# A LoRA projection: longer first loads, and GpSimd takes every second rounding

## The chip, the cores and the metric

The kernel runs on one core of a Trainium2 chip. The metric is the device time of one execution in microseconds (us). The kernel before took 163.57, 163.68 and 163.86 us in three runs; the median is 163.68 us. A core has five engines: TensorE (PE in the profile), VectorE (DVE), ScalarE (ACT), GpSimd (POOL) and SyncE (SP), which here does nothing but issue transfers and wait. Sixteen DMA engines move data between the chip's memory (HBM) and the on-chip buffer (SBUF).

## What is computed

```python
x_flat = x.reshape(-1, in_dim)            # 32768 x 256, float32
y = x_flat @ W                            # W: 256 x 256
lora_out = x_flat @ lora_A                # 256 x 16
lora_out = lora_out * lora_E              # 16 factors
lora_out = lora_out @ lora_B              # 16 x 256
y = y + scale * lora_out
```

The input is 33.6 MB and the output is as large. Everything else is small.

## The kernel before, in words

The kernel first folds the low-rank part into the weight: `weff = W + lora_A diag(lora_E) lora_B`, rounded to bf16 (lines 177 to 191 on VectorE, 238 to 246 on TensorE). After that, each output row is one product of an input row with `weff`.

The 32768 input rows are laid over 128 partitions, so a partition holds 256 rows of 256 numbers. "Rows" below means these: 8 rows are 1 MB of float32. They are cut into blocks (`BLOCKS`, line 11), and inside a block each partition's rows lie side by side in HBM, so that a load of n rows reads n KB in one piece for each partition (`rows_of`, line 97).

All rows go through one SBUF buffer, `ring`, which has room for 184 of the 256 rows (line 12). A load writes rows into the ring, the computation replaces them there by the results, and a store takes the results out. The last 72 rows use the places of the first 72, so their loads wait until the stores of those have landed.

The order of all large transfers is written out in `ORDER` (line 13): `L16` is a load of the next 16 rows, `S64` a store of the next 64, `W` the load of the weight. SyncE issues them in this order on one queue (lines 129 to 143). Before a load it waits for the stores whose places it takes (line 137); before a store it waits until ScalarE has counted up `s_c` (line 140). At the end it waits for the last stores (line 263). Every load has a semaphore of its own, `s_load`.

The computation goes in 32 steps of 8 rows, in two alternating sets of buffers:

- `rounded(n)` (line 158), on VectorE: round 8 rows from the ring to bf16, into `xb` (the cast of line 167). At the first step of a load it waits for that load (line 166).
- `transposes` (line 216), on TensorE: eight transposes (line 212) of `xb` into PSUM, `pt`. The two bf16 halves of a 32-bit word travel together, as float32.
- `copied(n)` (line 169), on VectorE: copy `pt` to SBUF, `xt` (line 172).
- `products` (line 222), on TensorE: sixteen products (line 228) of `xt` with `weff` into PSUM, `py`, in two halves of four rows.
- ScalarE copies each half from `py` back into the ring (line 202), and at the end of a store's rows it drains and counts up `s_c` (line 204).

TensorE's order is transposes of step n+1, then products of step n. So the results of step n come only after the input of step n+1 is there. VectorE's order is `copied(n)`, then `rounded(n+2)` (lines 193 to 195). GpSimd only builds the identity matrix for the transposes (lines 145 and 147) at the start.

Of the kernel before, what the change touches and what calls it, by code (L numbers as in the profile page):

```python
# [10 lines left out]
BLOCKS = [64, 32, 64, 24, 40, 32]  # L11
RING = 184
ORDER = [
    "L8", "W", "L8", "L16", "L16", "L16", "L16", "L16", "L24", "L24", "L16", "L24",
    "S64", "S32",
    "L8", "L16", "L16", "L16", "L16",  # L16
    "S64", "S24", "S40", "S32",
# [1 line left out]
G = 8  # L19
# [4 lines left out]
def kernel(  # L24
# [10 lines left out]
    nc = tc.nc  # L35
# [25 lines left out]
    xbs = [const.tile([P, G, K], BF16, name=f"xb_{i}") for i in range(2)]  # L61
# [23 lines left out]
    s_load = {f: sem(f"load_{f}") for f, _ in loads}  # L85

    s_last = sem("stores")
    s_store = {f: sem(f"store_{f}") for f, _ in stores if f < ROWS - RING}
# [4 lines left out]
    s_t, s_m, s_c = sem("s_t"), sem("s_m"), sem("s_c")  # L93
    k_x, k_t, k_y = ([sem(f"{k}_{i}") for i in range(2)] for k in ("k_x", "k_t", "k_y"))
    s_setup = sem("s_setup")

    def rows_of(flat, f, n):
        first, rows = block_of[f]
        block = flat[first * P:(first + rows) * P, :].rearrange("(p b) k -> p b k", b=rows)
        return block[:, f - first:f - first + n, :]  # L100

    def place(f, n):
        return ring[:, f % RING:f % RING + n, :]

    steps = list(range(0, ROWS, G))
    NS = len(steps)
# [5 lines left out]
    def load(f, n):  # L112
        return nc.sync.dma_start(out=place(f, n), in_=rows_of(x_flat, f, n)).then_inc(s_load[f], 16)
# [12 lines left out]

    with tc.tile_critical():  # L127

        for kind, f, n in queue[1:]:
            if kind == "W":  # L130
                nc.sync.dma_start(
                    out=w_sb, in_=W.rearrange("(p c) m -> p c m", c=KC)
                ).then_inc(s_w, 16)
            elif kind == "L":
                for g, m in stores:
                    if g < f + n - RING and f - RING < g + m and g in s_store:
                        nc.sync.wait_ge(s_store.pop(g), 16)
                load(f, n)
            elif kind == "S":
                nc.sync.wait_ge(s_c, stores.index((f, n)) + 1)  # L140
                nc.sync.dma_start(out=rows_of(out_flat, f, n), in_=place(f, n)).then_inc(
                    s_store.get(f, s_last), 16
                )

        nc.gpsimd.memset(ident_f, 0.0).then_inc(s_setup, 1)  # L145
        nc.gpsimd.wait_ge(s_setup, 1)
        nc.gpsimd.affine_select(  # L147
            out=ident_f,
            in_=ident_f,
            compare_op=mybir.AluOpType.not_equal,  # L150
            fill=1.0,
            base=0,
            pattern=[[-1, P]],
            channel_multiplier=1,
        ).then_inc(s_setup, 1)


        def rounded(n):

            if n == NS:  # L160

                nc.vector.sem_inc(k_x[n % 2], 1)
            if n >= NS:
                return
            if steps[n] in s_load:
                nc.vector.wait_ge(s_load[steps[n]], 16)
            nc.vector.tensor_copy(out=xbs[n % 2], in_=place(steps[n], G)).then_inc(k_x[n % 2], 1)  # L167

        def copied(n):

            nc.vector.wait_ge(s_t, n + 1)
            nc.vector.tensor_copy(  # L172
                out=xts[n % 2].rearrange("p g r c -> p (g r c)"),
                in_=pts[n % 2].rearrange("p g r -> p (g r)").bitcast(BF16),
            ).then_inc(k_t[n % 2], 1)

        nc.vector.wait_ge(s_in, 48)
        nc.vector.tensor_copy(out=b_bf, in_=b_sb)  # L178
        nc.vector.wait_ge(s_setup, 3)
        nc.vector.tensor_scalar(  # L180
            out=ate,
            in0=ps_at,
            scalar1=e_sb,
            scalar2=float(scale),
            op0=mybir.AluOpType.mult,
            op1=mybir.AluOpType.mult,
        ).then_inc(s_setup, 1)
        rounded(0)
        nc.vector.wait_ge(s_w, 16)
        nc.vector.wait_ge(s_setup, 5)  # L190
        nc.vector.tensor_add(out=weff, in0=w_sb, in1=ps_aeb).then_inc(s_setup, 1)  # L191
        rounded(1)
        for n in range(NS):
            copied(n)
            rounded(n + 2)


        for k in k_y:
            nc.scalar.sem_inc(k, 1)
        for h in range(ROWS // H):  # L200
            nc.scalar.wait_ge(s_m, h + 1)
            nc.scalar.copy(out=place(h * H, H), in_=pys[h % 2]).then_inc(k_y[h % 2], 1)  # L202
            if (h + 1) * H in store_ends:
                nc.scalar.drain().then_inc(s_c, 1)  # L204


        def take(token):
            nc.tensor.wait_ge(token, 1).then_inc(token, -1)  # L208


        def transpose(b, j):
            return nc.tensor.transpose(  # L212
                pts[b][:, j, :], xbs[b][:, j, :].bitcast(FP32), ident_f
            )

        def transposes(b):
            take(k_x[b])
            for j in range(G):
                t = transpose(b, j)
            t.then_inc(s_t, 1)  # L220

        def products(b):
            take(k_t[b])
            for j in range(G):
                if j % H == 0:
                    take(k_y[j // H])
                for c in range(KC):
                    m = nc.tensor.matmul(  # L228
                        pys[j // H][:, j % H, :],
                        xts[b][:, j, :, c],  # L230
                        weff[:, c, :],
                        start=(c == 0),
                        stop=(c == KC - 1),
                    )
                if j % H == H - 1:
                    m.then_inc(s_m, 1)

        nc.tensor.wait_ge(s_setup, 2)
        nc.tensor.wait_ge(s_in, 48)
        for c in range(KC):  # L240
            t = nc.tensor.transpose(ps_at[:, c, :], a_sb[:, c, :], ident_f)  # L241
        t.then_inc(s_setup, 1)
        nc.tensor.wait_ge(s_setup, 4)
        for c in range(KC):
            m = nc.tensor.matmul(ps_aeb[:, c, :], ate[:, c, :], b_bf, start=True, stop=True)  # L245
        m.then_inc(s_setup, 1)
        transposes(0)
        nc.tensor.wait_ge(s_setup, 6)
        left = nc.tensor.alloc_register("left")
        nc.tensor.reg_mov(left, NS // 2)  # L250
        with nc.tensor.While(left):
            transposes(1)
            products(0)
            transposes(0)
            products(1)
            nc.tensor.reg_sub(left, left, 1)

        total = nc.sync.alloc_register("total")
        nc.sync.reg_mov(total, n_last)
# [39 lines left out]
```

## Time and profile before

| What | Value |
| --- | --- |
| profiled execution, whole | 163.49 us |
| its span on the engines | 161.7 us |
| median of three runs | 163.68 us |
| TensorE, matmuls | 91.0 us busy (56%), 780 instructions |
| VectorE | 76.4 us busy (47%), 67 instructions |
| ScalarE | 63.1 us busy (39%), 65 instructions |
| GpSimd | 0.7 us busy, 6 instructions |
| VectorE's casts, line 167 | 32 of 1220 ns |
| VectorE's copies, line 172 | 32 of 1221 ns |
| data moved | 67.42 MB, mean 417 GB/s over the span |
| DMA packets | 3522 |

The span runs from the first to the last instruction of the profile; the whole execution has 1.8 us more around it. The page gives, for each engine, how long it was busy, the busy share in 40 equal slices of the span, the DMA queues, the chain of work that ended last, and groups of like instructions with their mean duration and the idle time before them. Views of the trace behind the page give the same by time: the order of one engine's instructions, what it waited for, and sums over chosen stretches. "X <- Y" in a list of waits reads "X waited for Y". SPq is SyncE's queue of commands, ACTq ScalarE's.

### The profile page before, as it was taken

To read this page: it belongs to the slowest core of one execution; us is meant where nothing else is said; L and a number is where in the kernel's file an instruction comes from. 1 tells how busy PE (TensorE), PEld (TensorE's weight loads), DVE (VectorE), ACT (ScalarE), POOL (GpSimd) and SP (SyncE) were. 2 spreads that over 40 slices of the span, in tenths; PEclk is the share of its full clock that TensorE was granted. 3 is DMA by queue.
4 is the path that set the end of the run, shared out by engine and by line. 5 is a ranking of instruction groups with operands and counts; after the bars stand their busy time and mean duration, and the time that the engine had idled before them with its cause. 6 is when DMAs were issued, how large, how long until landed. Compare 5 with 4: busy or idle time off the path is not lost. (4 is left out here: it accounts for less than half of the span.)

```text
span 161.7 us, 1972 instructions
## 1 busy us (share of the span) xinstructions
PE 91.0 (56%) x780; PEld 81.5 (50%) x780; DVE 76.4 (47%) x67; ACT 63.1 (39%) x65; POOL 0.7 (0%) x6
## 2 busy tenths in 40 slices
PE   0188999999999999970000079999994000000000
PEld 0066899999799999960000066999993000000000
DVE  0296999985889988800000048999930000000000
ACT  3004486868586868680000005768685000000000
POOL 1000000000000000000000000000000000000000
PEclk9999999999999999996555558999999555555555
DMA  5999999999999999799699999999899799899992
GB/s 179 417 426 450 413 434 442 417 458 426 432 415 438 432 521 456 324 519 470 300 413 407 440 421 446 424 421 571 357 486 470 340 395 488 381 466 442 405 421 113
DMA packets 3522, 67.42 MB, mean 417 GB/s; under 512 B 560, under 2 KB 576, under 8 KB 704
## 3 DMA queue, kind: packets, MB, share of 16 engines
q1 hardware_dynamic: 3312, 67.37, 97.6%
q10 hardware_dynamic: 208, 0.03, 0.1%
q14 instruction: 2, 0.02, 0.0%
HBM read 33.85 MB, written 33.55 MB: 417 GB/s over the span
## 5 line engine op out<-in xcount | busy, mean ns | idle before, releaser
L202 ACT COPY ring<-py 128x1024 f32<-128x1024 f32 x64 | 61.8, 1017 | 58.6 <-PE py L228 58.5
L228 PE MATMUL py<-weff,xt 128*128 128x256 bf16 x512 | 62.2, 275 | 0.7 <-PEq L208 0.7
L228 PEld LDWEIGHTS py<-weff,xt 128*128 128x128 bf16 x512 | 50.5, 99 | 7.4 <-issue 1.5
L167 DVE CAST xb<-ring 128x2048 bf16<-128x2048 f32 x32 | 39.0, 1220 | 31.8 <-DMA ring<-in_x_dram 31.5
L212 PE MATMUL pt<-ident_f,xb 128*128 128x128 f32 x264 | 36.7, 286 | 24.0 <-PEq L208 23.9
L212 PEld LDWEIGHTS pt<-ident_f,xb 128*128 128x128 f32 x264 | 31.7, 148 | 25.9 <-issue 25.6
L172 DVE COPY xt<-pt 128x2048 bf16<-128x2048 bf16 x32 | 39.1, 1221 | 4.5 <-PE pt L212 4.4
L241 PE MATMUL py<-ident_f,a_sb 128*16 128x128 f32 x2 | 0.6, 396 | 6.8 <-DMA b_sb<-in_lora_B_dram 6.8
L241 PEld LDWEIGHTS py<-ident_f,a_sb 128*16 128x16 f32 x2 | 0.1, 88 | 6.8 <-issue 6.8
L178 DVE CAST b_bf<-b_sb 16x256 bf16<-16x256 f32 x1 | 0.3, 282 | 6.7 <-DMA b_sb<-in_lora_B_dram 6.7
L202 ACT ACT_TABLE_LOAD x1 | 1.3, 1283 | 2.4 <-issue 2.4
L245 PE MATMUL py<-b_bf,ate 16*128 16x256 bf16 x2 | 0.6, 402 | 0.6 <-DVE ate L180 0.6
L180 DVE TENSOR_SCALAR ate<-py,e_sb 16x256 bf16<-16x256 f32 x1 | 0.5, 472 | 0.5 <-PE py L241 0.5
L191 DVE TENSOR_TENSOR weff<-w_sb,py 128x512 bf16<-128x512 f32 x1 | 0.7, 669 | 0.0
L245 PEld LDWEIGHTS py<-b_bf,ate 16*128 16x128 bf16 x2 | 0.1, 104 | 1.1 <-DVE ate L180 1.1
L147 POOL TENSOR_SCALAR_AFFINE_SELECT ident_f<-ident_f 128x128 f32<-128x128 f32 x1 | 0.3, 294 | 0.2 <-POOL ident_f L145 0.2
L145 POOL MEMSET ident_f<- 128x128 f32 x1 | 0.2, 205 | 1.0 <-SPq L127 1.0
L280 POOL MEMSET const-bfloat16-1.0<- 128x1 bf16 x1 | 0.1, 102 | 0.0
L280 POOL MEMSET const-uint8-127<- 128x1 uint8 x1 | 0.1, 102 | 0.0
L280 POOL MEMSET const-float32-0.0<- 128x1 f32 x1 | 0.1, 99 | 0.2 <-issue 0.2
L280 POOL MEMSET const-float32-1.0<- 128x1 f32 x1 | 0.1, 99 | 0.0
## 6 DMA issues: line engine op xcount, KB each, us to landing
ring<-in_x_dram SPq DMA_DIRECT2D x10, 2048.0 KB, 21.3
ring<-in_x_dram SPq DMA_DIRECT2D x3, 3072.0 KB, 42.5
out_dram<-ring SPq DMA_DIRECT2D x2, 4096.0 KB, 40.0
out_dram<-ring SPq DMA_DIRECT2D x1, 5120.0 KB, 37.4
ring<-in_x_dram SPq DMA_DIRECT2D x3, 1024.0 KB, 7.2
out_dram<-ring SPq DMA_DIRECT2D x1, 3072.0 KB, 39.1
w_sb<-in_W_dram SPq DMA_DIRECT2D x1, 256.0 KB, 5.1
out_dram<-ring SPq DMA_DIRECT2D x2, 43.1
```

The lines of the kernel that those rows point to most:

```text
L147: nc.gpsimd.affine_select(out=ident_f, in_=ident_f, compare_op=mybir.AluOpType.not_equal, fill=1.0, base=0, pattern=[[-1, P]], channel_mul ...
L167: nc.vector.tensor_copy(out=xbs[n % 2], in_=place(steps[n], G)).then_inc(k_x[n % 2], 1)
L172: nc.vector.tensor_copy(out=xts[n % 2].rearrange("p g r c -> p (g r c)"), in_=pts[n % 2].rearrange("p g r -> p (g r)").bitcast(BF16),).the ...
L178: nc.vector.tensor_copy(out=b_bf, in_=b_sb)
L180: nc.vector.tensor_scalar(out=ate, in0=ps_at, scalar1=e_sb, scalar2=float(scale), op0=mybir.AluOpType.mult, op1=mybir.AluOpType.mult,).the ...
L191: nc.vector.tensor_add(out=weff, in0=w_sb, in1=ps_aeb).then_inc(s_setup, 1)
L202: nc.scalar.copy(out=place(h * H, H), in_=pys[h % 2]).then_inc(k_y[h % 2], 1)
L212: return nc.tensor.transpose(pts[b][:, j, :], xbs[b][:, j, :].bitcast(FP32), ident_f)
L228: m = nc.tensor.matmul(pys[j // H][:, j % H, :], xts[b][:, j, :, c], weff[:, c, :], start=(c == 0), stop=(c == KC - 1),)
L241: t = nc.tensor.transpose(ps_at[:, c, :], a_sb[:, c, :], ident_f)
L245: m = nc.tensor.matmul(ps_aeb[:, c, :], ate[:, c, :], b_bf, start=True, stop=True)
L280: nc = _bacc.Bacc("TRN2", target_bir_lowering=False, num_devices=1)
```

## The change

The first load stretch, 184 rows, is cut into eight loads instead of eleven: 8, 8, 16, four of 32 and one of 24 rows, where it was 8, 8, five of 16, two of 24, one of 16 and one of 24. All other loads and stores stay.

From step 3 on, GpSimd does the rounding of the odd steps, 15 of the 32 casts; VectorE keeps the even ones and steps 0 and 1. GpSimd's cast of step n waits until the transposes of step n-2 are done, since they read the same `xb`, and, at its first use of a load, for that load. Each of the two engines waits once for each load that it reads. What SyncE waits for does not change: the list `freed` only keeps track of the stores that it has already waited for.

```diff
 ORDER = [
-    "L8", "W", "L8", "L16", "L16", "L16", "L16", "L16", "L24", "L24", "L16", "L24",
+    "L8", "W", "L8", "L16", "L32", "L32", "L32", "L32", "L24",
     "S64", "S32",
     "L8", "L16", "L16", "L16", "L16",
     "S64", "S24", "S40", "S32",
...
+        freed = []
...
-                    if g < f + n - RING and f - RING < g + m and g in s_store:
-                        nc.sync.wait_ge(s_store.pop(g), 16)
+                    if g < f + n - RING and f - RING < g + m and g not in freed:
+                        freed.append(g)
+                        nc.sync.wait_ge(s_store[g], 16)
...
-        def rounded(n):
-
-            if n == NS:
-
-                nc.vector.sem_inc(k_x[n % 2], 1)
-            if n >= NS:
-                return
-            if steps[n] in s_load:
-                nc.vector.wait_ge(s_load[steps[n]], 16)
-            nc.vector.tensor_copy(out=xbs[n % 2], in_=place(steps[n], G)).then_inc(k_x[n % 2], 1)
+        seen = []
+
+        def caster(n):
+            return nc.gpsimd if n % 2 == 1 and n >= 3 else nc.vector
+
+        def rounded(n, engine):
+            piece = max(f for f in s_load if f <= steps[n])
+            waits = [(s_load[piece], 16)]
+            for sem_, count in waits:
+                if (engine, sem_) not in seen:
+                    seen.append((engine, sem_))
+                    engine.wait_ge(sem_, count)
+            engine.tensor_copy(out=xbs[n % 2], in_=place(steps[n], G)).then_inc(k_x[n % 2], 1)
+
+
+        for n in range(NS):
+            if caster(n) is nc.gpsimd:
+                nc.gpsimd.wait_ge(s_t, n - 1)
+                rounded(n, nc.gpsimd)
+
...
         for n in range(NS):
             copied(n)
-            rounded(n + 2)
+
+            if n + 2 < NS and caster(n + 2) is nc.vector:
+                rounded(n + 2, nc.vector)
+            elif n + 2 == NS:
+
+                nc.vector.sem_inc(k_x[NS % 2], 1)
```

## The prediction, as it was put on record before the changed kernel ran

> **What bounds the kernel now.** I read the slices of the span and the queue table first. In the slices each digit is the busy share of the 16 DMA engines in tenths; the queue line gives packets, MB and share of the engines' time.
>
> ```profile
> DMA  5999999999999999799699999999899799899992
> ...
> q1 hardware_dynamic: 3312, 67.37, 97.6%
> ```
>
> One queue, filled by SyncE, is busy all the way from the first slice to the last. Next the chain that ended last, by engine:
>
> ```profile
> PE 14%; ACT 1%; ACTq 1%; issue 0%
> ```
>
> It accounts for 16% of the span and stops at 124.1 us, where the last store is issued; what follows belongs to the transfers. So I went on to SyncE's own waits (total, times, longest):
>
> ```profile
> SPq L141 <- ACTq L204: 70.2, 5, 26.9
> SPq L113 <- DMA out_dram<-ring: 39.6, 2, 33.4
> SPq L263 <- DMA out_dram<-ring: 35.8, 1, 35.8
> ```
>
> The first line is harmless: SyncE waits for results while its queue is still full of loads. The other two show transfers as the limit: the second load stretch waits for room in the ring, and the end waits for the last store. To see how early that store is, its issue (start, duration) and, from the window 91 to 130, KB and time from issue to landing of the last two stores:
>
> ```profile
> 124.14 0.33 SPq L141 DMA_DIRECT2D out_dram<-ring  x1
> ```
>
> ```profile
> out_dram<-ring SPq DMA_DIRECT2D x1, 5120.0 KB, 37.4
> out_dram<-ring SPq DMA_DIRECT2D x1, 4096.0 KB, 36.5
> ```
>
> The store of 40 rows (issued at 113.67) lands at 113.67 + 37.4 = 151.1, the store of 32 at 124.14 + 36.5 = 160.6, and only then is the queue empty. The last store's data cannot move before 151.1. The very first load (issued 0.74, 8 rows) landed 5.1 us later, and 8 rows take 2.45 us at the pace found below, so an issue must lead its data by 2.65 us: the last store could be issued as late as 148.5. **Compute has 24.4 us of cover.** The stretches of 10 us (busy per engine, clock, DMA share, GB/s) say that compute does not slow the transfers:
>
> ```profile
> 80.00:90.00 10.00, 0.00 (x0) 0.00 (x0) 0.00 (x0) 0.00 (x0) 0.00 (x0) 0.50 0.99 424
> ...
> 100.00:110.00 10.00, 9.87 (x91) 9.20 (x92) 9.44 (x9) 6.72 (x8) 0.00 (x0) 1.00 1.01 432
> ```
>
> With every compute engine idle the queue moves 424 / 0.99 = 428 GB/s per busy share, with all at work 432 / 1.01 = 428.
>
> **Part 1: eight loads for eleven.** The bytes are the same, so only the cost of a load beside its bytes can change. VectorE's timeline shows landings, since these casts wait for them (start, duration, in brackets the idle time before):
>
> ```profile
> 18.86 1.23 DVE L167 CAST xb<-ring 128x2048 bf16<-128x2048 f32 x1 [0.27 <-DMA ring<-in_x_dram]
> ...
> 23.76 1.23 DVE L167 CAST xb<-ring 128x2048 bf16<-128x2048 f32 x1 [0.28 <-DMA ring<-in_x_dram]
> ...
> 40.85 1.23 DVE L167 CAST xb<-ring 128x2048 bf16<-128x2048 f32 x1 [1.85 <-DMA ring<-in_x_dram]
> ...
> 48.16 1.23 DVE L167 CAST xb<-ring 128x2048 bf16<-128x2048 f32 x1 [0.41 <-DMA ring<-in_x_dram]
> ```
>
> Two loads of 16 rows land 23.76 - 18.86 = 4.90 us apart, two of 24 rows 48.16 - 40.85 = 7.31 us apart. The difference, 2.41 us for 8 rows, is 0.3013 us a row and leaves 4.90 - 16 x 0.3013 = 0.08 us per load. Three loads fewer: **-0.24 us**. No load of 32 rows is in this trace, so bounds. Before, 96 of the affected rows come in loads of 16 (6 x 4.90) and 72 in loads of 24 (3 x 7.31): 51.33 us. After, one load of 16 and one of 24 take 12.21 us, and 128 rows remain. At the 16-row pace (0.306 a row) they take 39.2, in all 51.41: +0.08. At the pace of the last store (160.64 - 151.07 = 9.57 us for 32 rows, 0.299) they take 38.3, in all 50.5: -0.8. The fit gives 4 x (32 x 0.3013 + 0.08) = 38.9, in all 51.1. I take the fit, being from loads of the same direction, and keep +0.08 and -0.8; the low end is a store's pace and far less likely.
>
> SyncE issues three DMAs fewer (0.33 to 1.94 us each, the last ending at 8.5 while the queue holds work to 60.3): nothing. Its waits before loads and stores stay where they were.
>
> **What the coarser loads make late.** Steps 4, 8, 12 and 16 now wait for a whole load of 32. Rows 16 to 32 land at 13.97 as before; then every 9.7 us: 23.7, 33.4, 43.1, 52.9, and the 24 rows at 60.2. Step 4 starts at 23.7 instead of 18.86, 4.8 us late. A step takes 2.62 us on TensorE (0.87 of transposes, 1.75 of products in the chain), so step 8 starts at 34.2, a little after its load. In the trace the first store is issued 35.40 - 28.66 = 6.74 us after step 8's cast starts: now at 40.9. Its cover is the load queue, which lasts to 6.54 + 53.8 = 60.3; less 2.65 that is 57.7. The second store slips from 46.6 to about 50.4 and is needed by 80.35 - 2.65 = 77.7. Should TensorE's clock drop in the gap (after the long idle stretch one step took 1.94 + 2.99 us), 2.3 us more still fit. Cost 0; without cover it would be about 5 us.
>
> **Part 2: GpSimd rounds every odd step from 3.** The trace has no such cast on GpSimd. Its two nearest rows (busy, mean ns):
>
> ```profile
> L147 POOL TENSOR_SCALAR_AFFINE_SELECT ident_f<-ident_f 128x128 f32<-128x128 f32 x1 | 0.3, 294 | 0.2 <-POOL ident_f L145 0.2
> L145 POOL MEMSET ident_f<- 128x128 f32 x1 | 0.2, 205 | 1.0 <-SPq L127 1.0
> ```
>
> Both do 128 elements a partition, the cast 2048; a memset of one element takes 0.10 us. The memset scales to 0.10 + 16 x 0.105 = 1.8 us; the select, scaled whole, to 16 x 0.294 = 4.7 us, and with 0.10 fixed to 3.2. I take 3.2, since the select reads and writes as a cast does, and keep 1.8 and 4.7. VectorE loses 15 x 1.22 = 18.3 us, which ended no wait that matters: 0.
>
> The new wait: the cast of step n waits for the transposes of n-2, and the transposes of n for the cast. Between them TensorE has products, transposes and products, 1.75 + 0.87 + 1.75 = 4.37 us. At 3.2 it is hidden; at 4.7 a pair of steps grows by some 0.4 us. Queued behind it on GpSimd is only the next cast; TensorE waits for it, then ScalarE, then the store. From 23.7 on 14 casts remain (steps 5 to 31): 14 x 0.4 = 6 us, inside the 24.4. Cost 0 at either bound.
>
> A page speaks against this part: the Trainium skill, "SBUF — State Buffer", section "Who interferes with whom", says that a VectorE copy or cast in a two-port mode and a GpSimd instruction exclude each other for the whole instruction. No row of before has GpSimd busy beside a cast; by that rule each cast would wait at most one VectorE cast, 1.22 us, so 4.7 becomes 5.9. That would use up to 14 x 1.6 = 22 us of the cover and leave the sum as it is; with it the first rival below would begin at a cast of 6.2 us instead of 7.4, and I would give it 0.06 instead of 0.04.
>
> **Sum.** -0.24 + 0 + 0. The profiled execution took 163.49 us (span 161.7 and 1.8 around it), which gives 163.25; it lies 0.19 below the median of the runs, 163.68, so in their terms 163.44. That is -0.15%; this kernel's measurement can tell about 0.2% (0.33 us) from no change.
>
> **Rivals.**
> *GpSimd becomes the bound (slower).* If its cast takes T beyond the slack, a pair of steps takes T + 0.87 + some 0.1. The last store is issued 124.14 - 115.79 = 8.35 us after the last cast ends, so it is late when 23.7 + 14 (T + 0.97) + 8.35 passes 148.5: from T = 7.4 us. Every us beyond costs 14: at 9.4, twice the upper row, 163.4 + 28 = 191. Against it: both rows; for it: nothing but the missing row. 0.04.
> *Large loads move worse (slower).* The first store of 64 rows took 80.35 - 60.34 = 20.0 us, 0.313 a row. Were 128 rows of load at that pace instead of 0.304, the time would be 163.44 + 1.1 = 164.6. Against it: the two load sizes get better with size, and that store follows a change of direction. 0.07.
> *Large loads move at the store pace (faster).* -0.8, or any gain above 0.33 us: 0.11 us per load removed would do. 162.8 to 163.3. For it: the 0.08 is a difference of two differences, uncertain by 0.05. 0.28.
> *A load's start is exposed on the queue (faster).* If each removed load freed the first load's 2.65 us, 3 x 2.65 = 8 us, 155.5. Against it: landings 4.90 us apart for 2 MB are 428 GB/s, the rate of the whole queue, without gaps. 0.01. The Trainium skill, "DMA: Bandwidth & Descriptors", section "Anatomy of one DMA — SWDGE (gpsimd) path", gives about 2.0 us fixed per transfer (for GpSimd's path), an estimate of 6 us for three if nothing hid it; 4.90 us between landings is less than its 2.0 plus 4.8 for the bytes, so the trace disagrees for queued loads.
> *The edit does not do what it says.* The instruction order shows 15 casts on GpSimd and loads of 8, 8, 16, 4 x 32, 24: left out.
>
> **How the numbers follow.** Forecast (within 0.2%) 0.60; faster 0.28 + 0.01, slower 0.04 + 0.07. Range: from 162.95 (most of the faster case) to 164.0 (the +0.08 bound and the runs' scatter of about 0.2); beyond it lie the two slower rivals, the exposed start and the far end of the store pace, together under 0.2.
>
> **What would show it.** Right: the queue's line again near 97.6% of a span of 161.3 to 161.7 with 384 packets and 48 semaphore writes fewer; casts of step 4 and 8 at about 23.7 and 34; the last store issued before 148.5 and landing near 160.4; GpSimd casts of 1.8 to 4.7 us. Wrong: a slice with DMA clearly under 9 before 150 us, a last store issued after 148.5, or loads of 32 landing more than 9.8 or less than 9.6 us apart.

## The result, and the profile after

The changed kernel is slower: 164.00 us median (20 runs, 163.66 to 164.40) against 163.62 us for the kernel before (20 runs beside it). One of those 20 took 342.97 us and is left out of the ratio, which is one of means. The ratio is 1.0021, with a 95% interval of 1.0015 to 1.0027: +0.34 us, where -0.24 us was forecast. Its profiled execution took 164.17 us with a span of 162.4 us; the one of before took 163.49 us. The two profiles thus stand 0.68 us apart, twice that difference, so single terms are read from them with care.

First the page of the changed kernel, slices and queue:

```profile
DMA  5999999999998999799699999999799699999990
...
q1 hardware_dynamic: 2880, 67.37, 97.2%
```

The queue is nearly as full as before (97.2% for 97.6%) and carries the same bytes in 432 packets fewer (384 of data, 48 semaphore writes), and still the span is longer. SyncE's waits:

```profile
SPq L143 <- ACTq L221: 78.5, 5, 35.9
SPq L280 <- DMA out_dram<-ring: 36.2, 1, 36.2
SPq L113 <- DMA out_dram<-ring: 35.5, 2, 28.1
```

The first store waits longer for its results (35.9 for 26.9): it is issued 6.2 us later, and SyncE is done issuing loads 2.8 us earlier. The ring and the end still wait for stores: no new bound. The last store's issue, and the last two stores' KB and time to landing:

```profile
124.37 0.33 SPq L143 DMA_DIRECT2D out_dram<-ring  x1
```

```profile
out_dram<-ring SPq DMA_DIRECT2D x1, 5120.0 KB, 37.8
out_dram<-ring SPq DMA_DIRECT2D x1, 4096.0 KB, 37.0
```

The last store is issued only 0.23 us later than before and lands at 161.4 instead of 160.6. It is not late; the queue ahead of it is. Next GpSimd's timeline (start, duration):

```profile
14.14 2.87 POOL L172 CAST xb<-ring 128x2048 bf16<-128x2048 f32 x1 [11.95 <-DMA ring<-in_x_dram]
...
30.91 1.89 POOL L172 CAST xb<-ring 128x2048 bf16<-128x2048 f32 x1 [4.19 <-PE pt L229]
...
113.69 1.89 POOL L172 CAST xb<-ring 128x2048 bf16<-128x2048 f32 x1 [3.22 <-PE pt L229]
```

and VectorE's at the first load of 32 rows:

```profile
23.74 1.23 DVE L172 CAST xb<-ring 128x2048 bf16<-128x2048 f32 x1 [6.01 <-DMA ring<-in_x_dram]
```

The casts are cheap, and step 4 starts at 23.7, as forecast. What differs is how much is computed beside the first stores. The stretch 60 to 80 us, busy time and instructions of TensorE, its weight loads, VectorE, ScalarE and GpSimd, before:

```profile
60.00:80.00 20.00, 11.62 (x107) 10.53 (x104) 7.73 (x7) 9.64 (x10) 0.00 (x0) 0.85 0.91 394
```

and after:

```profile
60.00:80.00 20.00, 17.14 (x157) 15.65 (x155) 11.68 (x10) 13.49 (x14) 3.79 (x2) 1.00 0.97 418
```

The sum of the instructions is 228 before and 338 after: 110 more run while the first store of 64 rows moves. The experiments ask whether this is the cost.

### The profile page after: what moved, and what is told of

Read it like the earlier page. It is cut to its first block, busy times and chain, and to the rows that moved or that the text cites. A ratio compares the mean times of both kernels' runs of the same rounds, so it can differ in the third digit from the quotient of the medians.

```text
span 162.4 us, 1980 instructions
## 1 busy us (share of the span) xinstructions
PE 92.3 (57%) x780; PEld 82.5 (51%) x780; DVE 59.9 (37%) x52; ACT 63.1 (39%) x65; POOL 32.7 (20%) x21
## 3 DMA queue, kind: packets, MB, share of 16 engines
q1 hardware_dynamic: 2880, 67.37, 97.2%
## 5 line engine op out<-in xcount | busy, mean ns | idle before, releaser
L245 PE MATMUL py<-weff,xt 128*128 128x256 bf16 x512 | 63.6, 279 | 0.5 <-PEq L225 0.4
L172 POOL CAST xb<-ring 128x2048 bf16<-128x2048 f32 x15 | 32.0, 2130 | 81.4 <-DMA ring<-in_x_dram 45.2
L172 DVE CAST xb<-ring 128x2048 bf16<-128x2048 f32 x17 | 20.7, 1219 | 30.5 <-DMA ring<-in_x_dram 30.4
```

The lines of the kernel that those rows point to most:

```text
L172: engine.tensor_copy(out=xbs[n % 2], in_=place(steps[n], G)).then_inc(k_x[n % 2], 1)
L245: m = nc.tensor.matmul(pys[j // H][:, j % H, :], xts[b][:, j, :, c], weff[:, c, :], start=(c == 0), stop=(c == KC - 1),)
```

## The experiments

**First round: which part costs?** Theory A: the new cut of the loads. B: GpSimd's casts. C: the computation that is later. All four kernels ran on one chip beside the kernel before (163.65 us).

The changed kernel again:

> The changed kernel again, beside the three others on one chip. All theories expect a ratio of 1.002 (1.0015 to 1.0027 was measured). In the profile: loads of 32 rows 9.7 us apart, the last load of 24 rows landing 7.6 us after the one before it (7.3 in the kernel before), one DMA engine up to 1 us behind the others at the end.

Measured: 164.20 us, 1.0031 (1.0018 to 1.0045). The loss is there again.

The loads alone. The edits of this run and of the next two are shown against the changed kernel:

```diff
-            return nc.gpsimd if n % 2 == 1 and n >= 3 else nc.vector
+            return nc.vector
```

> The eight loads, with all casts on VectorE. Theory A (the new cut of the loads costs the time, at the end of the last load) expects 1.002 and the last load landing 7.6 us after the one before. Theory B (GpSimd's casts slow the transfers) expects the gain of the prediction alone, 0.9985 (-0.24 us), and the last load after 7.3 us. Theory C (the later computation is what costs) expects 1.002, since the coarse loads make it late here too.

Measured: 164.05 us, 1.0023 (1.0014 to 1.0031). B falls.

GpSimd's casts alone:

```diff
-    "L8", "W", "L8", "L16", "L32", "L32", "L32", "L32", "L24",
+    "L8", "W", "L8", "L16", "L16", "L16", "L16", "L16", "L24", "L24", "L16", "L24",
```

> The eleven loads of before, with every second cast on GpSimd. Theory A expects 1.000. Theory B expects 1.002 to 1.0035 (the measured loss, or that and the 0.24 us that the fewer loads gained). Theory C expects 1.000, since nothing is late.

Measured: 163.74 us, 1.0006 (0.9997 to 1.0014). This run keeps GpSimd's casts and has the loads of before. GpSimd's casts alone cost nothing that can be told from zero.

Neither, but the computation late (loads of before, all casts on VectorE, both edits as above):

```diff
...
-            piece = max(f for f in s_load if f <= steps[n])
-            waits = [(s_load[piece], 16)]
+            row = steps[n] if steps[n] < 32 or steps[n] >= 160 else steps[n] // 32 * 32 + 24
+            pieces = sorted({max(f for f in s_load if f <= r) for r in (steps[n], row)})
+            waits = [(s_load[f], 16) for f in pieces]
```

> The eleven loads and VectorE's casts of before, but steps 4, 8, 12 and 16 wait also for the load that ends 32 rows further on, so that the computation is as late as in the changed kernel. Theories A and B expect 1.000, theory C 1.002. First store issued near 41 us instead of 35.4 by all.

Measured: 164.08 us, 1.0026 (1.0015 to 1.0036). **A falls, C holds**: with the loads and the casts of before, lateness alone gives the whole loss, though every store is issued long before its turn. Its stretch holds 151 instructions more than before:

```profile
60.00:80.00 20.00, 19.21 (x176) 17.60 (x174) 14.53 (x13) 15.15 (x16) 0.00 (x0) 1.00 0.92 399
```

**How lateness can cost without a late store.** The packet records of the trace show it. They do not name the DMA engine, but each packet of an engine starts where its last one ended, so they can be followed as 16 chains. A packet of a store of 64 rows holds 64 KB and takes 2418 ns. On one of the 16 engines it takes about 136 ns more, and only while the compute engines work; it is called the slow engine below. Its packets of the first store, start in us and duration in ns:

```text
before   61.97 2545   64.51 2573   67.08 2554   69.63 2531   then 2418   (TensorE ends at 71.6)
changed  62.34 2564   64.90 2564   67.46 2549   70.01 2573   72.58 2545   75.12 2535   (TensorE ends near 77)
```

In the store of 64 rows after the second load stretch it is the same: in the kernel before 111.15 2545, 113.69 2578, 116.27 2554, 118.82 2554, 121.36 2516, 123.87 2465, 126.33 2418; TensorE ends at 123. That chain runs on without a gap to the last packet of the kernel: the last store is complete when this engine is. The other engines are done earlier (before: fifteen by 160.4, the last at 160.7; changed: by 160.3 and 161.4).

Of these 0.67 us between the two traces, 0.30 come from the longer packets of the first store, and 0.37 were there when it began: the slow engine starts on it at 59.54 before and at 59.91 in the changed kernel. The second part scatters. It is 59.51 to 59.91 in the ten traces with eleven loads and the whole computation, and 59.76 to 59.91 in the three with eight loads. So a part of the loss, up to some 0.2 us, may still belong to the loads; these traces do not decide it.

**Second round: more lateness, and which engine.** Kernel before on this chip: 163.58 us. Later by 15.5 us (14 were meant); the edit is shown against the late kernel of the first round:

```diff
-            row = steps[n] if steps[n] < 32 or steps[n] >= 160 else steps[n] // 32 * 32 + 24
+            row = 88 if steps[n] == 32 else steps[n]
```

> Loads and casts of before, but step 4 waits until rows 88 to 95 have landed (33.5 us) as well, so that all steps of the first stretch are about 14 us later than before, twice to three times as late as in the changed kernel. Theory C with its mechanism (while the compute engines work beside a store, the transfers of the store slow down on one of the 16 DMA engines, by 2.55/2.42 = 5.6%, and the last store waits for that engine): 14 x 5.6% = 0.8 us, a ratio of 1.004 to 1.005, and the first store of 64 rows ending some 0.4 us later than in the kernel before. Rival (a fixed price, once the first store is issued later): 1.0025 as in the run that was 5 us late.

Measured: 164.47 us, 1.0059 (1.0047 to 1.0071). It is more than was expected, and TensorE ends at 87.1 instead of 71.6. The price grows with the lateness; a fixed price falls. The stretch now holds 536 instructions (before, 228 up to its end at 73):

```profile
60.00:90.00 30.00, 27.11 (x249) 24.96 (x246) 21.66 (x19) 21.20 (x22) 0.00 (x0) 1.00 0.94 406
```

Next, one engine alone beside the last stores, where nothing is computed otherwise. TensorE (the edits of all tails are shown against the kernel before):

```diff
...
+        nc.tensor.reg_mov(more, 17)
+        with nc.tensor.While(more):
+            for b in range(2):
+                for j in range(G):
+                    transpose(b, j)
+            nc.tensor.reg_sub(more, more, 1)
```

> The kernel before, and after the last product TensorE goes on with 272 idle transposes (to about 153 us), alone, while the last stores run. Theory C1 (TensorE's work is what slows the one DMA engine): 28 x 5.6% = 1.6 us, a ratio of 1.009 to 1.010. If it is another engine's work, 1.000.

Measured: 165.02 us, 1.0084 (1.0069 to 1.0099). Its stretch:

```profile
124.00:160.00 36.00, 28.68 (x263) 28.44 (x261) 0.00 (x0) 0.07 (x1) 0.00 (x0) 0.97 0.95 409
```

On the slow engine every packet from 124 to 152 is longer (40 KB packets 1575 to 1604 ns instead of 1514), and after that none. VectorE:

```diff
...
+        nc.vector.wait_ge(s_c, len(stores))
+        for n in range(24):
+            if n:
+                nc.vector.wait_ge(s_d, n)
+            if n % 2 == 0:
+                nc.vector.tensor_copy(out=xts[0]..., in_=pts[0]...).then_inc(s_d, 1)
+            else:
+                nc.vector.tensor_copy(out=xbs[1], in_=place(steps[NS - 1], G)).then_inc(s_d, 1)
```

> The kernel before, and after the last result VectorE goes on alone with 24 large copies and casts (to about 153 us), while the last stores run. Theory C2 (VectorE's work, or any engine's): 1.6 us, 1.009 to 1.010. If it is TensorE's or ScalarE's work, 1.000.

Measured: 163.77 us, 1.0009 (1.0000 to 1.0018). VectorE is as busy in this stretch as TensorE was:

```profile
124.00:160.00 36.00, 0.00 (x0) 0.00 (x0) 29.42 (x24) 0.77 (x1) 0.00 (x0) 0.54 0.95 410
```

ScalarE, in the same way with 28 copies from `pys` to `xts[0]`:

> The kernel before, and after the last result ScalarE goes on alone with 28 copies of 128x1024 from PSUM to SBUF (to about 153 us), while the last stores run. Theory C3 (ScalarE's work, or any engine's): 1.6 us, 1.009 to 1.010. If it is TensorE's or VectorE's work, 1.000.

Measured: 163.69 us, 1.0006 (0.9997 to 1.0015).

```profile
124.00:160.00 36.00, 0.00 (x0) 0.00 (x0) 0.00 (x0) 28.60 (x29) 0.00 (x0) 0.53 0.95 410
```

So it looked like TensorE alone; but TensorE had also issued 544 instructions, VectorE 24 and ScalarE 28.

**Third round: the work or the number of instructions?** Kernel before: 163.62 us. TensorE with long products instead of the transposes:

```diff
...
+        nc.tensor.reg_mov(more, 16)
...
+                nc.tensor.matmul(
+                    pts[b][:, 0:4, :].rearrange("p g r -> p (g r)"),
+                    ident_f,
+                    w_sb.rearrange("p c m -> p (c m)"),
...
```

> The kernel before with a tail of TensorE alone again, now 32 float32 products of 128x128 by 128x512, each several times longer than a transpose (estimate 0.9 us, 28 us in all), so that TensorE is as busy as in the tail of 272 transposes with far fewer instructions. Theory P (TensorE's being busy slows the one DMA engine): ratio 1.008 again. Theory N (the number of its instructions counts): under 1.003.

Measured: 164.07 us, 1.0025 (1.0016 to 1.0035). Each product was recorded as two matmuls and two weight loads, so 128 instructions:

```profile
L262 PE MATMUL pt<-w_sb,ident_f 128*128 128x512 f32 x64 | 27.6, 592 | 0.0
L262 PEld LDWEIGHTS pt<-w_sb,ident_f 128*128 128x128 f32 x64 | 12.1, 190 | 14.8 <-issue 14.8
```

TensorE was busy 27.6 us, about as long as with the transposes, at less than a third of the price. VectorE with small copies:

```diff
+        nc.vector.wait_ge(s_c, len(stores))
+        for b in range(2):
+            for n in range(160):
+                nc.vector.tensor_copy(out=xts[b]...[:, 8 * n:8 * n + 8], in_=w_sb[:, 0, 0:8])
```

> The kernel before with a tail of VectorE alone, 320 copies of 128x8 instead of 24 large ones, so that an engine other than TensorE issues some ten instructions a us beside the last stores. Theory N (the number of instructions of any engine counts): slower, about 1.005 if they take 20 us or more. Theory P (TensorE's work alone): 1.000.

Measured: 164.61 us, 1.0051 (1.0036 to 1.0066), with less VectorE time than the 24 large copies took:

```profile
124.00:160.00 36.00, 0.00 (x0) 0.00 (x0) 23.55 (x320) 0.12 (x1) 0.00 (x0) 0.56 0.95 407
```

In this trace the last engine is another one. It also carries the program's own instructions, on queue q14:

```profile
q14 instruction: 4, 0.03, 0.0%
```

Before, that line counts two, at 64.6 and 103.9 us. The two more, at 134.8 and 145.2, are of 8 KB and take 0.31 us each, and the packet of the store behind them takes 0.35 and 0.47 us longer. This engine lands at 162.13 and the slow engine at 161.51 (before: 160.69). So the time of this run is not the price of the copies alone, but the packets of the slow engine are longer here too.

**The number of instructions counts, not how long they keep an engine busy.** The table has two measures. "More us" is the ratio less 1, times the kernel before. "Longer packets" is by how much the packets of the slow engine exceed their usual duration in sum (2418 ns for 64 KB, 1514 for 40, 1213 for 32, 912 for 24), less the same sum of the kernel before (0.56 us in the first two stores, 0.06 from 123.9 us on). It is read from the one profiled execution of each kernel, in the first two stores for the upper five rows and from 123.9 us on for the tails:

| Kernel | more instructions beside stores | more us | longer packets, us | ns for one, from the packets |
| --- | --- | --- | --- | --- |
| changed | 110 | 0.34 (0.25 to 0.44) | 0.30 | 2.7 |
| changed, again | 121 | 0.51 (0.29 to 0.74) | 0.33 | 2.8 |
| loads alone | 106 | 0.38 (0.23 to 0.51) | 0.29 | 2.7 |
| late | 151 | 0.43 (0.25 to 0.59) | 0.43 | 2.8 |
| later by 15.5 us | 308 | 0.97 (0.77 to 1.16) | 0.85 | 2.8 |
| 272 transposes | 544 | 1.37 (1.13 to 1.62) | 1.35 | 2.5 |
| 32 long products | 128 | 0.41 (0.26 to 0.57) | 0.36 | 2.8 |
| 320 small copies | 320 | 0.83 (0.59 to 1.08) | 0.75 | 2.3 |
| 24 large copies | 24 | 0.15 (0.00 to 0.29) | 0.07 | 2.9 |
| 28 copies of ScalarE | 28 | 0.10 (-0.05 to 0.25) | 0.08 | 3.0 |

From 24 instructions to 544, each adds 2.3 to 3.0 ns to the packets of the slow engine. In the traces of the small copies and of the 24 large ones another engine is the last, so the time there holds more than these packets. TensorE and VectorE were each tried with many short instructions and with few long ones; ScalarE only with few, and GpSimd not alone.

The same eleven loads, sorted by size:

```diff
-    "L8", "W", "L8", "L16", "L16", "L16", "L16", "L16", "L24", "L24", "L16", "L24",
+    "L8", "W", "L8", "L16", "L16", "L16", "L16", "L16", "L16", "L24", "L24", "L24",
```

> The kernel before with its eleven loads in another order: 8, 8, six of 16, three of 24. VectorE's wait of 1.85 us at row 96 should go, so that the first stretch is computed some 0.5 us earlier. By the mechanism that is 0.03 us less, too little to see: ratio 0.9995 to 1.000. If the slips of the computation cost more than 5.6% of themselves, a gain shows.

Measured: 163.58 us, 0.9993 (0.9984 to 1.0002): no difference that can be measured, as expected of so little. And the other direction, with 7 of 8 transposes and 12 of 16 products of each step left out:

```diff
-            for j in range(G):
+            for j in range(G - 1, G):
...
-                for c in range(KC):
+                for c in range(KC if j % H == H - 1 else 0):
...
```

> The kernel before, leaving out 7 of 8 transposes and 12 of 16 products of each step, so that TensorE is done soon after each load and idle beside most of the stores. By the mechanism the 12 + 11 us of TensorE's work beside stores in the kernel before cost 23 x 5.6% = 1.3 us; less TensorE work gives back most of it: 162.4 to 162.9, ratio 0.993 to 0.996. If the late computation costs by another way (the time at which stores are issued, say), 0.998 to 1.000.

Measured: 163.02 us, 0.9960 (0.9945 to 0.9976): **faster, by removing work that no store was late for**. It is less than the full 1.3 us, and a little less than was expected: in this trace no engine ends alone any more (160.17, the next at 160.16), so others than the slow engine now set the end.

**Fourth round: do the fewer loads gain anything?** With few instructions beside the stores, eleven loads against eight.

> The kernel before with 7 of 8 transposes and 12 of 16 products left out, again, as the partner of the next run. Expected 0.996 as measured.

> The same with the eight loads of the changed kernel, all casts on VectorE. If the loss of the changed kernel is the instructions that run later beside a store, little of it is left here (5 us later at some 6 instructions a us is 0.07 us), and the 0.24 us that the prediction expected of three loads fewer should come out: 0.9985 to 0.999 of its partner. If the three loads bring nothing to the end, the two are equal; if large loads themselves cost time, it is slower, 1.001 or more of its partner.

Measured: 163.16 us, 0.9972 (0.9963 to 0.9982), and 163.18 us, 0.9975 (0.9965 to 0.9984). The two are equal; between their intervals a gain of about 0.15 us could hide, the forecast 0.24 us hardly. In both traces the slow engine is not the last one, so this pair says nothing of what eight loads do to that engine.

## Why the prediction was wrong, point by point

- **What bounds the kernel.** Right in kind: the queue stays full, no store is issued late, and the last store is issued at 124.4 with 24 us of cover. But the queue was taken as one thing that ends at one time. It is 16 engines, and the last store is complete when the last of them is.
- **"Compute does not slow the transfers."** Wrong, and it carries the rest. It rested on 428 GB/s in two stretches. The one with all engines at work held loads; the stretch with stores held no computation. And 428 is a mean over 16 engines, from shares printed to two digits: one engine that is 5.6% slower moves it by 0.35%, too little to see there.
- **Part 1, the loads.** The price was right, and the gain did not last. Loads of 32 land 9.71 us apart (forecast 9.7). From the landing of row 32 to that of row 160 it takes 39.06 to 39.11 us in the twelve traces with eleven loads and 38.85 or 38.86 in the four with eight: 0.23 us less, for 0.24 forecast. But the last load of 24 rows then takes longer behind loads of 32: 7.67 to 7.83 us as a mean of the 16 engines, for 7.31 to 7.52. In the trace of the changed kernel the last load has landed at 60.48, before at 60.34. The fourth round finds no gain at the end.
- **"What the coarser loads make late … Cost 0."** This is the step that failed. The slip was sized rightly (step 4 at 23.7, first store issued at 41.6 for 40.9 forecast), and as a delay of stores it is hidden. It costs because 110 instructions move from beside loads to beside the first store, where they make the packets of the slow engine longer by 0.30 us in sum, of the 0.34 measured.
- **Part 2, GpSimd.** Cost 0, right. The cast takes 1.89 us, near the lower bound, not 3.2. Where a VectorE cast has begun before it, it takes up to 2.88: at 14.14 it starts 0.1 us after one and ends at 17.01, 1.75 us after that cast's end, while VectorE keeps its 1.23. In the four other places where the two meet it is the same, 1.74 or 1.75 us. The Trainium skill, "SBUF — State Buffer", section "Who interferes with whom", has it that, when VectorE works in a two-port mode, the one of the two that issues first keeps the shared ports for its whole instruction, and the other is blocked. These five places agree.
- **The rivals.** None was it. Large loads were not slower by pace, and GpSimd was far from its 7.4 us. The first store did follow at 0.313 us a row in the trace of before, which was put down to a change of direction. In that trace its last packet belongs to the engine that carries the instructions: one packet took 2849 ns behind such a load at 64.6 us. The slow engine was done 0.4 us before it, though its packets are 0.55 us longer in sum there.
- **The range.** 164.00 us is its upper end. That end was made of a slower pace of the loads and of the scatter, and neither is what happened, so that the time came so near was luck.

What stays open: why one DMA engine alone is slowed, and what the instructions send that gets in its way. The Trainium skill, "NOTIFIC — the notification-queue block", section "The AWS profiler on NQ 0", says that under the profiler all five engines write records of the starts and ends of their instructions to HBM. A price for each instruction, on stores above all, would fit that, but all runs here were recorded, and none shows the time without it. So it is not shown that the price would be there without the recording. Open too is why the last load of the first stretch takes longer behind loads of 32 rows.

## What to carry to other kernels

When the transfers are the bound, look at the slowest DMA engine and not at their mean, and ask of every slip of the computation what it then runs beside, even where its store has 20 us to spare. Here, in runs that were all recorded, an instruction beside a store made the packets of one engine 2.3 to 3.0 ns longer, on TensorE and VectorE alike, so fewer and larger instructions, or instructions beside loads, were worth more than a shorter busy time. A rate is evidence only for the pairing in which it was read: loads with computation say nothing of stores with computation.

## What was not expected of the hardware

One DMA engine of 16 is 5.6% slower on stores (64 KB in about 2554 ns instead of 2418) while TensorE issues some 18 instructions a us, and back to 2418 within a packet when it stops. 320 VectorE copies of 128x8 made its packets longer by 0.75 us in sum, 24 copies of 128x2048 by 0.07, though the latter kept VectorE busy longer. An 8 KB load of the program's own instructions takes 0.31 us of one engine, and the packet behind it was 0.33 to 0.48 us longer in nearly all traces. Between 57 and 59 us, at the end of the first load stretch, load packets of 24 KB take up to 1227 ns before and up to 1775 ns after, instead of 914; no run here explains it.
